# Column sums for the norms by VectorE adds and one full product, and chunks of 512 tokens in panels that feed no norm

## The chip, the cores and the metric

One core of one Trainium2 chip runs the whole program in one launch. The metric is the time on the device in microseconds, as the median of several runs.

## What is computed

Two blocks of a model with 1024 channels over 1024 tokens, all in float32. The first block (with 16 meta tokens in front) mixes by a state space layer and a gated recurrence, and ends in a gated feed-forward net. The second half is two residual layers, "ab" (multiscale pooling and a chunked gating unit) and "cd" (Fourier mixing and attention over the tokens and 256 context tokens). Around the change stand the norms, which need sums over the 1024 channels of each token:

```python
def _layer_norm(x, g, b):
    xf = x.astype(jnp.float32)
    mu = jnp.mean(xf, axis=-1, keepdims=True)
    var = jnp.mean(jnp.square(xf - mu), axis=-1, keepdims=True)
    return ((xf - mu) * lax.rsqrt(var + EPS) * g + b).astype(x.dtype)
...
def _post_norm(x, y, gate, g, b):
    return _layer_norm(ALPHA * x + gate * y, g, b)
...
def rmsnorm(x, g):
    xf = x.astype(jnp.float32)
    y = xf * lax.rsqrt(jnp.mean(xf * xf, axis=-1, keepdims=True) + EPS)
    return (y * g.astype(jnp.float32)).astype(x.dtype)
...
        h = h + merged @ w_out[l]
        z = rmsnorm(h, ffn_norm_g[l])
        u = causal_dwconv(z @ w_up[l], conv_w[l], conv_b[l])
        h = h + (jax.nn.silu(u[..., :D_FF]) * u[..., D_FF:]) @ w_down[l]
    return rmsnorm(h[:, N_META:], final_norm_g)
```

## The kernel before, in words

Activations lie with 128 channels on the partitions and the tokens along the free dimension, so 1024 channels are eight tiles. A product of matrices is made of panels (`panel`): a panel is one output tile of 128 channels, whose columns are cut in chunks of tokens. `CHX` is three chunks of 384, 256 and 384; `CHJ` the same for the 1026 tokens of the first block. For each chunk a PSUM bank is taken from a pool of four (`ps_mm`), 8 (or 4) tiles of the contraction are multiplied into it and an eviction takes the result away. Each factor is kept as a sum of two reduced-precision parts, and each contraction tile costs three matmul instructions (`mm3`, recorded at L83), so a panel of eight tiles is 24 instructions in each chunk, 72 in all. Weights come by DMA and are split in their two parts by ACT (L75) and DVE (L76). Activations are split in the same way by `split_act` (L741, L742).

A sum over channels runs across partitions, so it is a product with ones on PE. `col_sum` gathers the eight source tiles of a chunk in groups of four: each is multiplied with a 32-column matrix of ones (L813), four tiles side by side into one PSUM bank; then ACT copies the bank (L817) and a product with `sel` (L818) adds the four parts and spreads the sum over all partitions. With `tail` set, the last source goes straight into that last bank by a full 128-column product of ones (L808). These products take plain float32 sources, and one of them is recorded as two matmul instructions. Some sums are formed otherwise: `closing` adds the first tiles on DVE into an accumulator (`aacc`, `cacc`, `sqacc`), and with `sq` set (the merge) it uses full products of ones for the accumulator (L779) and for each of the last tiles (L792).

Where the sums are taken:

- **The merge** (`closing` with `sq`, three last panels): the norm in front of the feed-forward net.
- **`ffn.down`, last call**: for each chunk the eight output tiles (L949, evicted with the residual at L951), squared by ACT (L963), a column sum, the reciprocal root (L106 on ACT, L108 to L111 on DVE), and `x1_chunk`, which scales the chunk (L986), modulates it and splits it into `hx`, the input of ab_x. The other nine calls of `down` feed no norm.
- **The context path** (`ctx_path`, 256 tokens): sums of `x` and, in `ln_chunk`, of its squares.
- **ab_x** (`half_out(1)` through `closing`, six last panels, eviction L1309) and **cd_close** (`closing`, seven last panels, eviction L1684): for each chunk the sum of the values, and then `ln_chunk`: mean (L1042), subtraction (L1045), squares (L1047), their column sum, root, and `emit`. The last chunk (`c == 2`) has `tail` set.

What sets the order: the program is written straight on, and a scheduler gives each engine a fixed order of its instructions. Each engine works through its own list, so an instruction that waits holds up all behind it. Products of the next stage or panel are placed between the parts of a sum.

Of the kernel before, what the change touches and what calls it, by code (L numbers as in the profile page):

```python
# [21 lines left out]
CHX = [(0, 384), (384, 640), (640, 1024)]  # L22
NC5 = 130
# [14 lines left out]
class Build:  # L38
# [715 lines left out]
    def closing(self, wsrc, X, nk, chunks, evac, r, sq, acc, tp, done, nres=3, xpool=None, npan=8):  # L754
        nc = self.nc
        n0 = npan - nres
        for i in range(n0):
# [11 lines left out]
            self.panel(w, X, nk, chunks, ev)  # L769
# [5 lines left out]
        for c, (lo, hi) in enumerate(chunks):  # L775
            n = hi - lo
            if sq:
                pc = self.ps_sm()[:, 0:n]
                nc.tensor.matmul(pc, self.ones, acc[:, lo:hi], start=True, stop=False)  # L779
            else:  # L780
                add = self.col_sum(nres + 1, n, lambda: tp.tile([128, 384], F32, tag="mu", name=self.nm("cse"), bufs=1), int(hi == chunks[-1][1]))
                add(0, acc[:, lo:hi])
            for j, (w, o) in enumerate(ws):
# [119 lines left out]
    def ffn(self):  # L903
# [5 lines left out]
        with ExitStack() as es:  # L909
# [32 lines left out]
            def down(js, last):  # L942
# [9 lines left out]
                if not last:  # L952
                    for o in range(8):
                        for lo, hi in CHX:
                            one(o, lo, hi)
                    return
                for c, (lo, hi) in enumerate(CHX):
                    n = hi - lo
                    add = self.col_sum(8, n, lambda: tp.tile([128, 384], F32, tag="cse", name=self.nm("cse"), bufs=1), int(c == 2))
                    for o in range(8):  # L960
                        one(o, lo, hi)
                        t = tp.tile([128, 384], F32, tag="tmp", name=self.nm("sqt"), bufs=6)[:, 0:n]
                        nc.scalar.activation(t, h1[o][:, 2 + lo:2 + hi], AF.Square)  # L963
                        pc = add(o, t)
# [73 lines left out]
    def ln_chunk(self, tp, r, ps, n, emit, sqt, tail):  # L1038
# [4 lines left out]
        add = self.col_sum(8, n, lambda: tp.tile([128, 384], F32, tag="mu", name=self.nm("cse"), bufs=1), tail)  # L1043
        for k in range(8):
# [3 lines left out]
            ps = add(k, t)  # L1048
# [21 lines left out]
    def ab_mixer(self, tp, yp, X, T, chunks, half_out, fill):  # L1070
# [6 lines left out]
        for g, w_ in enumerate((2, 4, 8, 16)):  # L1077
            ap = tile_("ap", T + 16, 2)
# [33 lines left out]
        ys = []  # L1112
# [45 lines left out]
    def ctx_path(self):  # L1158
# [8 lines left out]
        with ExitStack() as es:  # L1167
# [45 lines left out]
            self.ab_mixer(tp, yp, X, T, CH, half_out, fill)  # L1213
# [612 lines left out]
```

## Time and profile before

| what | value |
|---|---|
| median of three runs | 3195.61 us (3192.84 to 3197.05) |
| the profiled execution's own time | 3194.65 us |
| its span | 3192.9 us |
| mean granted TensorE clock | 0.994 |
| PE busy | 3109.1 us (97%) |
| DVE busy | 1830.5 us (57%) |
| ACT busy | 1121.4 us (35%) |

The engines are PE (matmuls), PEld (weight loads, which run beside PE), DVE (VectorE), ACT (ScalarE), POOL (GpSimd) and SP (queues of DMAs). Busy time counts the instructions on an engine; the chain is the work that ended last, followed back from the end step by step to what released it. The granted clock is a share of full speed: 1.00 is 2.4 GHz and 0.50 is 1.2 GHz. A window's row gives each engine's busy time with the number of its instructions. Matmuls overlap in their records, so the price of one is read from the distance between starts, or from a long stretch divided by its count.

### The profile page before, as it was taken

How to read it: one execution, taken by the hardware profiler on the slowest of the kernel's cores; microseconds unless marked ns; L12 is line 12 of the kernel's file. 1: busy time of each engine (PE TensorE's matmuls, PEld its weight loads, DVE VectorE, ACT ScalarE, POOL GpSimd, SP SyncE). 2: the span in 40 equal slices, each digit the busy share in tenths (PEclk: the TensorE clock that was granted, in tenths of full speed). 3: DMA queues.
4: the chain of work that ended last, by engine and by line, in shares of the span. 5: the costliest groups of instructions: out<-in, count | busy, mean ns of one | idle time of the engine just before them, and what ended most of it. 6: DMA issues, size and time to landing. Idle time of an engine off the chain costs nothing.

```text
span 3192.9 us, 47786 instructions
## 1 busy us (share of the span) xinstructions
PE 3109.1 (97%) x19986; PEld 2838.8 (89%) x19986; DVE 1830.5 (57%) x3508; ACT 1121.4 (35%) x1846; POOL 93.1 (3%) x99
## 2 busy tenths in 40 slices
PE   8999899999999999999999999999999999999998
PEld 6999887878999999999999999979999798856576
DVE  7549477776455435365555555555444646688844
ACT  5342642333345312142222122243121535445542
POOL 0000000000210000000000000000000000022100
PEclk9999999999999999999999999999999999999999
DMA  5352445343452234211111111101111314200111
GB/s 158 89 163 94 141 170 168 113 139 108 142 170 93 63 129 132 67 40 48 48 50 41 47 53 47 47 24 59 47 50 37 104 61 136 90 4 11 67 63 53
DMA packets 106384, 269.01 MB, mean 84 GB/s; under 512 B 14798, under 2 KB 43694, under 8 KB 105974
## 3 DMA queue, kind: packets, MB, share of 16 engines
q1 hardware_dynamic: 99656, 245.35, 23.6%
q10 hardware_dynamic: 4464, 16.34, 1.3%
q0 software_dynamic: 2048, 4.26, 0.6%
q8 instruction: 157, 2.57, 0.3%
q14 instruction: 59, 0.48, 0.0%
HBM read 219.12 MB, written 46.11 MB: 83 GB/s over the span
## 4 chain that ended last, share of the span: by engine, by line
PE 87%; DVE 6%; ACT 3%; DMA 3%; issue 1%; SPq 0%; DVEq 0%; ACTq 0%
PE mm L83 63%; PE mm L949 7%; PE mm L1567 3%; PE sm L813 2%; PE sm L1555 2%; PE mm L1124 2%; DMA YBd<-o 1%; PE sm L1531 1%; ACT Tt L502 1%; DVE R L604 1%; PE sm L465 1%; DMA wm<-ab_w_mod 0%; PE sm L708 0%; PE sm L1017 0%; PE sm L687 0%
## 5 line engine op out<-in xcount | busy, mean ns | idle before, releaser
L83 PE MATMUL mm<-z,whl 128*128 128x256 f32 (+3 forms) x4032 | 684.5, 325 | 1.9 <-ACT z L231 1.0
L83 PE MATMUL mm<-a,whl 128*128 128x384 f32 (+1 forms) x4320 | 682.6, 319 | 1.6 <-ACT u L917 1.6
L83 PEld LDWEIGHTS mm<-a,whl 128*128 128x128 f32 x4320 | 678.5, 188 | 3.7 <-ACT u L917 1.9
L83 PEld LDWEIGHTS mm<-z,whl 128*128 128x128 f32 x4032 | 639.1, 190 | 36.0 <-issue 29.2
L76 DVE TENSOR_TENSOR whl<-wraw,whl 128x1024 fp32r<-128x1024 f32 (+2 forms) x258 | 302.8, 1179 | 224.5 <-ACT whl L75 223.7
L75 ACT CAST whl<-wraw 128x1024 fp32r<-128x1024 f32 (+2 forms) x258 | 260.6, 1015 | 342.1 <-PE mm L949 136.9
L83 PE MATMUL mm<-hx,whl 128*128 128x384 f32 (+1 forms) x2232 | 365.4, 322 | 7.7 <-ACT fx L1378 7.1
L83 PEld LDWEIGHTS mm<-hx,whl 128*128 128x128 f32 x2232 | 351.2, 189 | 16.8 <-ACT fx L1378 7.3
L949 PEld LDWEIGHTS mm<-g,whl 128*128 128x128 f32 x1584 | 248.0, 188 | 13.9 <-issue 8.1
L949 PE MATMUL mm<-g,whl 128*128 128x384 f32 (+1 forms) x1584 | 257.9, 322 | 2.3 <-DVE f L951 1.2
L83 PE MATMUL mm<-b,whl 128*128 128x384 f32 (+1 forms) x1152 | 180.9, 319 | 0.0
L83 PEld LDWEIGHTS mm<-b,whl 128*128 128x128 f32 x1152 | 180.8, 189 | 0.0
L917 ACT COPY u<-mm 128x384 f32<-128x384 f32 x132 | 58.4, 445 | 317.9 <-PE mm L83 317.9
L951 DVE TENSOR_TENSOR f<-f,mm 128x384 f32<-128x384 f32 (+1 forms) x240 | 118.4, 509 | 71.3 <-PE mm L949 70.4
L83 PEld LDWEIGHTS mm<-y,whl 128*128 128x128 f32 x816 | 119.9, 188 | 13.0 <-issue 9.8
L83 PE MATMUL mm<-y,whl 128*128 128x256 f32 (+1 forms) x816 | 127.8, 312 | 1.3 <-ACT y L741 1.0
L1567 PE MATMUL mm<-m,KB 97*128 97x512 f32 x420 | 118.2, 401 | 1.3 <-ACT P L1568 1.3
L1568 ACT ACTIVATE P<-mm 128x512 f32<-128x512 f32 x160 | 91.5, 596 | 68.6 <-PE mm L1567 50.9
L1532 DVE TENSOR_REDUCE mx<-sm 128x1 f32<-128x512 f32 (+1 forms) x192 | 103.8, 596 | 15.6 <-PE sm L1531 14.6
L1567 PEld LDWEIGHTS mm<-m,KB 97*128 97x128 f32 x420 | 76.9, 191 | 24.9 <-issue 7.3
L923 DVE TENSOR_SCALAR av<-u,conv_w,conv_b 128x1024 f32<-128x1024 f32 x22 | 17.9, 812 | 138.9 <-ACT u L917 138.9
L923 DVE TENSOR_SCALAR ag<-u,conv_w,conv_b 128x1024 f32<-128x1024 f32 x22 | 17.9, 813 | 119.1 <-ACT u L917 119.1
(519 smaller groups left out, 3729.9 us busy)
## 6 DMA issues: line engine op xcount, KB each, us to landing
wraw<-w_up SPq DMA_DIRECT2D x44, 512.0 KB, 3.2
wraw<-w_h SPq DMA_DIRECT2D x32, 512.0 KB, 3.4
wraw<-ab_w SPq DMA_DIRECT2D x32, 512.0 KB, 3.3
wm<-ab_w_mod SPq DMA_DIRECT2D x24, 512.0 KB
wm<-cd_w_mod SPq DMA_DIRECT2D x24, 512.0 KB, 4.8
wraw<-w_down SPq DMA_DIRECT2D x22, 512.0 KB, 3.2
ut<-Ud SPq DMA_DIRECT2D x16, 520.0 KB, 4.0
gt<-Gd SPq DMA_DIRECT2D x16, 513.0 KB, 3.2
```

Of the source, the lines that this page charges most:

```text
L75: self.nc.scalar.copy(t[:, 0], raw)
L76: self.nc.vector.tensor_tensor(out=t[:, 1], in0=raw, in1=t[:, 0].bitcast(F32), op=ALU.subtract)
L83: nc.tensor.matmul(ps, W[:, wp, wofs + 128 * k:wofs + 128 * k + 128], X(xp, kofs + k, lo, hi), start=first and k == 0 and i == 0, stop=las ...
L813: nc.tensor.matmul(p4[32 * j:32 * j + 32], self.ones[:, 0:32], x, start=i < 4, stop=i - len(pend) + j + 5 >= m)
L917: return u, (self.split_w(A["w_up"][p], [1024]), lambda c, lo, hi, ps: nc.scalar.copy(u[:, lo:hi], ps))
L949: nc.tensor.matmul(ps, ws[j][:, wp, 128 * o:128 * o + 128], G[j][:, xp, lo:hi], start=n_ == 0 and i == 0, stop=n_ == len(js) - 1 and i == 2)
L951: v.tensor_tensor(out=h1[o][:, 2 + lo:2 + hi], in0=h1[o][:, 2 + lo:2 + hi], in1=ps, op=ALU.add)
L1124: nc.tensor.matmul(ps, X(xp, k, 128 * t, 128 * t + 128), wv[k // 4][:, wp, 256 * (k % 4):256 * (k % 4) + 256], start=k == 0 and i == 0, st ...
L1532: v.tensor_reduce(out=mx[:, qt, j:j + 1], in_=ps, axis=mybir.AxisListType.X, op=ALU.max)
L1555: mm = nc.tensor.matmul(po[64 * c:64 * c + 64, :], vv(t)[:, 64 * h:64 * h + 64], P[t][:, c], start=t == 0, stop=t == KT - 1)
L1567: nc.tensor.matmul(ps, K[0:97, kp, 128 * t:128 * t + 128], Q[0:97, qp, 512 * c:512 * c + 512], start=i == 0, stop=i == 2)
L1568: E[t] = nc.scalar.activation(Pt[:, c], ps, AF.Exp, scale=scale)
```

## The change

Two edits. First, sums over the channels are added up on DVE and go through one full product of ones for each chunk: in `closing` (all last tiles are added to the accumulator; in the last chunk the last tile goes straight into the product's bank), in the last `ffn.down` (the squares are added into `cse`), in `ln_chunk` except for the last chunk and the first block, and in the context path's sum of values. Second, panels that feed no norm are cut in two chunks of 512 (`CH5`): in ab_x the pooling panels 1 to 3, the second half's eight and the first output half; the panels of `closing` ahead of its last ones; the nine inner calls of `down`; gates 1 to 7; three Fourier panels; two query panels; and the four of the Fourier output.

```diff
@@ closing
-    def closing(self, wsrc, X, nk, chunks, evac, r, sq, acc, tp, done, nres=3, xpool=None, npan=8):
+    def closing(self, wsrc, X, nk, chunks, evac, r, sq, acc, tp, done, nres=3, xpool=None, npan=8, wide=None):
...
-            self.panel(w, X, nk, chunks, ev)
+            self.panel(w, X, nk, wide or chunks, ev)
...
-            if sq:
-                pc = self.ps_sm()[:, 0:n]
-                nc.tensor.matmul(pc, self.ones, acc[:, lo:hi], start=True, stop=False)
-            else:
-                add = self.col_sum(nres + 1, n, lambda: tp.tile([128, 384], F32, tag="mu", name=self.nm("cse"), bufs=1), int(hi == chunks[-1][1]))
-                add(0, acc[:, lo:hi])
...
-                    nc.tensor.matmul(pc, self.ones, t, start=False, stop=i == npan - 1)
-                else:
-                    pc = add(j + 1, src)
+                    src = t
+                if i == npan - 1 and hi == chunks[-1][1]:
+                    nc.tensor.matmul(pc, self.ones, src, start=False, stop=True)
+                    continue
+                nc.vector.tensor_tensor(out=acc[:, lo:hi], in0=acc[:, lo:hi], in1=src, op=ALU.add)
+                if i == npan - (2 if hi == chunks[-1][1] else 1):
+                    pc = self.ps_sm()[:, 0:n]
+                    nc.tensor.matmul(pc, self.ones, acc[:, lo:hi], start=True, stop=i == npan - 1)
@@ ffn.down
-                        for lo, hi in CHX:
+                        for lo, hi in CH5:
                             one(o, lo, hi)
...
-                    add = self.col_sum(8, n, lambda: tp.tile([128, 384], F32, tag="cse", name=self.nm("cse"), bufs=1), int(c == 2))
+                    tot = tp.tile([128, 384], F32, tag="cse", name=self.nm("cse"), bufs=1)[:, 0:n]
...
-                        t = tp.tile([128, 384], F32, tag="tmp", name=self.nm("sqt"), bufs=6)[:, 0:n]
+                        t = tp.tile([128, 384], F32, tag="tmp", name=self.nm("sqt"), bufs=6)[:, 0:n] if o else tot
                         nc.scalar.activation(t, h1[o][:, 2 + lo:2 + hi], AF.Square)
-                        pc = add(o, t)
+                        if o == 7 and c == 2:
+                            nc.tensor.matmul(pc, self.ones, t, start=False, stop=True)
+                            continue
+                        if o:
+                            v.tensor_tensor(out=tot, in0=tot, in1=t, op=ALU.add)
+                        if o == (6 if c == 2 else 7):
+                            pc = self.ps_sm()[:, 0:n]
+                            nc.tensor.matmul(pc, self.ones, tot, start=True, stop=o == 7)
@@ ln_chunk
-            ps = add(k, t)
+            if tail:
+                ps = add(k, t)
+            elif k == 0:
+                t0 = t
+            else:
+                v.tensor_tensor(out=t0, in0=t0, in1=t, op=ALU.add)
+        if not tail:
+            ps = self.ps_sm()[:, 0:n]
+            nc.tensor.matmul(ps, self.ones, t0, start=True, stop=True)
@@ ctx_path
-            add = self.col_sum(8, T, lambda: tp.tile([128, 384], F32, tag="mu", name=self.nm("cse"), bufs=1))
-            for k in range(8):
-                ps = add(k, x[:, k])
...
+            tot = sqs[:, 0]
+            v.tensor_tensor(out=tot, in0=x[:, 0], in1=x[:, 1], op=ALU.add)
+            for k in range(2, 8):
+                v.tensor_tensor(out=tot, in0=tot, in1=x[:, k], op=ALU.add)
+            ps = self.ps_sm()[:, 0:T]
+            nc.tensor.matmul(ps, self.ones, tot, start=True, stop=True)
@@ gate, and alike in fourier, latents' input, the Fourier output, ab_mixer and half_out(0)
-        self.panel(w, X, 8, CHX, ev)
+        self.panel(w, X, 8, CH5, ev)
```

How the order moves is shown at three places. A row is an instruction in an engine's order, with its number there, the line, output and inputs, the shape and how many alike follow in a row (`f`: the residual; `hx`: ab_x's input; `mm`, `sm`: PSUM banks). The line numbers of the changed kernel run 1 to 22 ahead of those of before.

First, PE at the end of the FFN's last `down`, before:

```order
4575 L813 MATMUL sm_19587<-sqt_19671,ones 32x384
4576 L813 MATMUL sm_19587<-sqt_19687,ones 32x384
4577 L949 MATMUL mm_19711<-g_18997,whl_19191 128x384
4578 L813 MATMUL sm_19587<-sqt_19703,ones 32x384
4579 L949 MATMUL mm_19711<-g_18997,whl_19191 128x384
4580 L949 MATMUL mm_19711<-g_19178,whl_19196 128x384 x3
4581 L83 MATMUL mm_19808<-hx_19351,whl_19803 128x384 x2
4582 L83 MATMUL mm_19834<-hx_19351,whl_19803 128x256
4583 L818 MATMUL sm_19588<-cse_19708,sel 128x384
4584 L83 MATMUL mm_19834<-hx_19351,whl_19803 128x256
4585 L83 MATMUL mm_19808<-hx_19351,whl_19803 128x384
4586 L808 MATMUL sm_19588<-sqt_19725,ones 128x384
```

and in the changed kernel:

```order
4384 L951 MATMUL mm_19115<-g_18094,whl_18602 128x384 x3
4385 L951 MATMUL mm_19115<-g_18413,whl_18607 128x384 x3
4386 L951 MATMUL mm_19115<-g_18594,whl_18612 128x384 x3
4387 L84 MATMUL mm_19212<-hx_18763,whl_19207 128x384
4388 L973 MATMUL sm_19113<-cse_18995,ones 128x384
4389 L967 MATMUL sm_19113<-sqt_19129,ones 128x384
4390 L84 MATMUL mm_19212<-hx_18763,whl_19207 128x384 x2
```

The 32-column products among L949 (now L951) are gone. The full products of the sum (L973 for `cse`, L967 for the last square) now stand behind one product of the next stage.

Second, DVE at the same place, before:

```order
2402 L742 TENSOR_TENSOR hx_19355<-hx_19568,hx_19355 128x256
2403 L742 TENSOR_TENSOR hx_19356<-hx_19573,hx_19356 128x256
2404 L951 TENSOR_TENSOR f_13003<-f_13003,mm_19673 128x384
2405 L742 TENSOR_TENSOR hx_19357<-hx_19578,hx_19357 128x256
2406 L742 TENSOR_TENSOR hx_19358<-hx_19583,hx_19358 128x256
2407 L951 TENSOR_TENSOR f_13034<-f_13034,mm_19689 128x384
2408 L951 TENSOR_TENSOR f_13065<-f_13065,mm_19711 128x384
2409 L76 TENSOR_TENSOR whl_19803<-wraw_19804,whl_19803 128x1024
2410 L76 TENSOR_TENSOR whl_19887<-wraw_19888,whl_19887 128x1024
2411 L108 TENSOR_SCALAR rsm_19730<-sm_19588 128x384
2412 L109 TENSOR_TENSOR rsm_19730<-rsm_19730,rsy_19728 128x384
2413 L110 TENSOR_TENSOR rsm_19730<-rsm_19730,rsy_19728 128x384
```

and in the changed kernel:

```order
2367 L953 TENSOR_TENSOR f_13024<-f_13024,mm_19096 128x384
2368 L953 TENSOR_TENSOR f_13055<-f_13055,mm_19115 128x384
2369 L743 TENSOR_TENSOR hx_18769<-hx_18986,hx_18769 128x256
2370 L743 TENSOR_TENSOR hx_18770<-hx_18991,hx_18770 128x256
2371 L970 TENSOR_TENSOR cse_18995<-cse_18995,sqt_19025 128x384
2372 L970 TENSOR_TENSOR cse_18995<-cse_18995,sqt_19042 128x384
2373 L970 TENSOR_TENSOR cse_18995<-cse_18995,sqt_19059 128x384
2374 L970 TENSOR_TENSOR cse_18995<-cse_18995,sqt_19076 128x384
2375 L970 TENSOR_TENSOR cse_18995<-cse_18995,sqt_19093 128x384
2376 L970 TENSOR_TENSOR cse_18995<-cse_18995,sqt_19110 128x384
2377 L77 TENSOR_TENSOR whl_19207<-wraw_19208,whl_19207 128x1024
2378 L77 TENSOR_TENSOR whl_19291<-wraw_19292,whl_19291 128x1024
```

Six adds (L970) now stand between the last evictions (L953) or splits (L743) and the weight splits (L77) and root (L109).

Third, DVE in ab_x's closing, in the last chunk, before:

```order
2696 L1045 TENSOR_TENSOR f_13065<-f_13065,mu_22719 128x256
2697 L1309 SCALAR_TENSOR_TENSOR f_12803<-mm_22821,mod_ab,f_12803 128x384
2698 L1309 SCALAR_TENSOR_TENSOR f_12897<-mm_22835,mod_ab,f_12897 128x384
2699 L1309 SCALAR_TENSOR_TENSOR f_13003<-mm_22853,mod_ab,f_13003 128x384
2700 L1309 SCALAR_TENSOR_TENSOR f_13034<-mm_22867,mod_ab,f_13034 128x384
2701 L76 TENSOR_TENSOR whl_23020<-wraw_23021,whl_23020 128x1024
2702 L76 TENSOR_TENSOR whl_23026<-wraw_23027,whl_23026 128x1024
2703 L108 TENSOR_SCALAR rsm_22756<-sm_22722 128x256
2704 L1309 SCALAR_TENSOR_TENSOR f_13065<-mm_22886,mod_ab,f_13065 128x384
```

and in the changed kernel, the same evictions (now L1331):

```order
2660 L1063 TENSOR_TENSOR sqt_21587<-sqt_21587 128x256
2661 L793 TENSOR_TENSOR aacc<-aacc,f_12701 128x384
2662 L1063 TENSOR_TENSOR sqt_21587<-sqt_21587,sqt_21593 128x256
2663 L1331 SCALAR_TENSOR_TENSOR f_12795<-mm_21681,mod_ab,f_12795 128x384
2664 L1063 TENSOR_TENSOR sqt_21587<-sqt_21587,sqt_21593 128x256
2665 L793 TENSOR_TENSOR aacc<-aacc,f_12795 128x384
2666 L1063 TENSOR_TENSOR sqt_21587<-sqt_21587,sqt_21600 128x256
2667 L1331 SCALAR_TENSOR_TENSOR f_12889<-mm_21696,mod_ab,f_12889 128x384
2668 L1063 TENSOR_TENSOR sqt_21587<-sqt_21587,sqt_21600 128x256
2669 L793 TENSOR_TENSOR aacc<-aacc,f_12889 128x384
2670 L1063 TENSOR_TENSOR sqt_21587<-sqt_21587,sqt_21607 128x256
2671 L1331 SCALAR_TENSOR_TENSOR f_12993<-mm_21711,mod_ab,f_12993 128x384
```

The evictions stood together, and now adds for this chunk's values (L793) and for the squares of the second chunk (L1063) stand between them. Ahead of them, between the eviction of `f_12701` and that of `f_12795`, stand 30 rows of the first two chunks' norms.

## Rows read from the trace of the kernel before

**Rows 1.** The page, parts 1 and 4: busy time by engine; the chain by engine.
```profile
PE 3109.1 (97%) x19986; PEld 2838.8 (89%) x19986; DVE 1830.5 (57%) x3508; ACT 1121.4 (35%) x1846; POOL 93.1 (3%) x99
...
PE 87%; DVE 6%; ACT 3%; DMA 3%; issue 1%; SPq 0%; DVEq 0%; ACTq 0%
```

**Rows 2.** Chain in order of time, stretches of products alone: start us, us, what.
```profile
1350.81 4.21 PE mm L83 x24
...
1477.52 22.78 PE mm L949 x144
...
2295.54 22.41 PE mm L1124 x192
...
2648.75 11.16 PE mm L1419 x48
...
2724.06 11.24 PE mm L83 x72
```

**Rows 3.** PE's timeline in the FFN's last down: start us, us, instructions.
```profile
2112.09 0.83 PE L813 MATMUL sm<-sqt,ones 128*32 128x384 f32 x2
2112.86 0.86 PE L949 MATMUL mm<-g,whl 128*128 128x256 f32 x5
2113.55 0.86 PE L818 MATMUL sm<-cse,sel 128*128 128x384 f32 x2
2113.95 2.25 PE L949 MATMUL mm<-g,whl 128*128 128x256 f32 x15
```

**Rows 4.** Windows, stages E, A, B, C, D: us, PE, PEld, DVE, ACT, POOL busy (x), PEclk.
```profile
970.40:981.50 11.10, 11.10 (x67) 6.57 (x68) 4.39 (x12) 5.46 (x13) 0.00 (x0) 1.00 0.00 0
1343.80:1403.90 60.10, 58.49 (x337) 54.47 (x336) 38.58 (x75) 23.72 (x44) 0.00 (x0) 1.00 0.10 35
2097.30:2155.40 58.10, 56.36 (x308) 42.52 (x308) 30.71 (x66) 30.17 (x64) 0.00 (x0) 1.00 0.03 7
2455.10:2520.30 65.20, 65.20 (x350) 45.25 (x349) 39.92 (x86) 32.10 (x68) 0.00 (x0) 1.00 0.19 65
...
3081.00:3171.90 90.90, 90.85 (x521) 71.87 (x520) 28.87 (x61) 18.72 (x40) 0.00 (x0) 1.00 0.08 30
```

**Rows 5.** PE's groups by line and shape, 2097.2 to 2155.4: busy us, mean ns | idle before.
```profile
L949 PE MATMUL mm<-g,whl 128*128 128x384 f32 x152 | 31.3, 350 | 1.5 <-DVE f L951 1.2 <-DVE g L742 0.3
L949 PE MATMUL mm<-g,whl 128*128 128x256 f32 x96 | 12.5, 287 | 0.0
```

**Rows 6.** DVE's timeline: two dependent operations, then eight independent ones.
```profile
2116.45 0.55 DVE L108 TENSOR_SCALAR rsm<-sm 128x384 f32<-128x384 f32 x1
2117.04 0.56 DVE L109 TENSOR_TENSOR rsm<-rsm,rsy 128x384 f32<-128x384 f32 x1
...
2467.35 3.84 DVE L1045 TENSOR_TENSOR f<-f,mu 128x384 f32<-128x384 f32 x8
```

**Rows 7.** Windows, inside and behind PE's longest idle stretch, same columns.
```profile
2529.00:2532.00 3.00, 0.00 (x0) 0.00 (x0) 3.00 (x8) 2.97 (x7) 0.00 (x0) 0.50 0.70 256
2532.00:2536.00 4.00, 3.52 (x18) 3.52 (x19) 1.14 (x5) 2.94 (x6) 0.00 (x0) 0.56 0.93 272
```

**Rows 8.** PE's groups of products, 2455.0 to 2520.4, same columns.
```profile
L83 PE MATMUL mm<-y,whl 128*128 128x384 f32 x110 | 22.3, 348 | 0.0
L83 PE MATMUL mm<-y,whl 128*128 128x256 f32 x72 | 11.3, 297 | 0.0
L83 PE MATMUL mm<-hx,whl 128*128 128x384 f32 x54 | 10.7, 348 | 0.0
...
L83 PE MATMUL mm<-hx,whl 128*128 128x256 f32 x13 | 3.0, 320 | 0.0
```

**Rows 9.** PE's timeline at that idle stretch; in brackets idle us and its releaser.
```profile
2532.48 0.80 PE L83 MATMUL mm<-hx,whl 128*128 128x256 f32 x2 [7.11 <-ACT fx L1378]
```

**Rows 10.** PE's timeline at the start of the last chunk of the last down.
```profile
2125.91 3.07 PE L949 MATMUL mm<-g,whl 128*128 128x384 f32 x16 [1.20 <-DVE f L951]
```

More of the change, by code (lines that the diff above doesn't have):

```diff
@@ L22 @@
 CHX = [(0, 384), (384, 640), (640, 1024)]
+CH5 = [(0, 512), (512, 1024)]
 NC5 = 130
@@ L1042, in ln_chunk @@
         v.tensor_scalar(out=mu, in0=ps, scalar1=1.0 / 1024, scalar2=None, op0=ALU.mult)
-        add = self.col_sum(8, n, lambda: tp.tile([128, 384], F32, tag="mu", name=self.nm("cse"), bufs=1), tail)
+        if tail:
+            add = self.col_sum(8, n, lambda: tp.tile([128, 384], F32, tag="mu", name=self.nm("cse"), bufs=1), tail)
         for k in range(8):
@@ L1047, in ln_chunk @@
             nc.scalar.activation(t, r(k), AF.Square)
-            ps = add(k, t)
+            if tail:
+                ps = add(k, t)
[6 more added lines that the diff above has]
+            nc.tensor.matmul(ps, self.ones, t0, start=True, stop=True)
         rs = self.rsqrt(tp, ps, n, 1.0 / 1024, EPS / ALPHA ** 2)
@@ L1068, in ab_consts, with ab_mixer @@
         nc.sync.dma_start(self.sgb, A["sgu_b"].partition_broadcast(128))
-    def ab_mixer(self, tp, yp, X, T, chunks, half_out, fill):
+    def ab_mixer(self, tp, yp, X, T, first, wide, half_out, fill):
         nc, A = self.nc, self.A
@@ L1077, in ab_mixer @@
         for g, w_ in enumerate((2, 4, 8, 16)):
+            chunks = wide if g else first
             ap = tile_("ap", T + 16, 2)
@@ L1111, in ab_mixer @@
         half_out(0, ys)
-        ys = []
+        ys, chunks = [], wide
         nt = T // 128
@@ L1212, in half_out @@
                     self.panel(w, Y, 4, CH, ev)
-            self.ab_mixer(tp, yp, X, T, CH, half_out, fill)
+            self.ab_mixer(tp, yp, X, T, CH, CH, half_out, fill)
             self.abg, self.abb = self.load(self.const, "ab_ln_g"), self.load(self.const, "ab_ln_b")
@@ L1220, in emit @@
                 self.split_act(H[:, :, k], 0, T, d)
-            add = self.col_sum(8, T, lambda: tp.tile([128, 384], F32, tag="mu", name=self.nm("cse"), bufs=1))
-            for k in range(8):
-                ps = add(k, x[:, k])
             sqs = cp.tile([128, 4, T], F32, name="csq")
-            self.ln_chunk(tp, lambda k: x[:, k], ps, T, emit, lambda k: sqs[:, k % 4], 0)
+            tot = sqs[:, 0]
[4 more added lines that the diff above has]
+            nc.tensor.matmul(ps, self.ones, tot, start=True, stop=True)
+            self.ln_chunk(tp, lambda k: x[:, k], ps, T, emit, lambda k: sqs[:, 1 + (k - 1) % 3 if k else 0], 0)
             for _ in range(16):
@@ L1314, in half_out @@
                 if which:
-                    self.closing(ws, Y, 4, CHX, ev, self.rx, False, acc, tp, done, nres=6)
+                    self.closing(ws, Y, 4, CHX, ev, self.rx, False, acc, tp, done, nres=6, wide=CH5)
                 else:
@@ L1320, in half_out @@
                         w = w2[:, :, 512 * (i % 2):512 * (i % 2) + 512]
-                        self.panel(w, Y, 4, CHX, lambda c, lo, hi, ps: ev(i, c, lo, hi, ps))
-            self.ab_mixer(tp, yp, X, 1024, CHX, half_out, lambda: None)
+                        self.panel(w, Y, 4, CH5, lambda c, lo, hi, ps: ev(i, c, lo, hi, ps))
+            self.ab_mixer(tp, yp, X, 1024, CHX, CH5, half_out, lambda: None)
     def cd_x(self):
@@ L1379, in fourier @@
             if h:
-                self.panel(w, X, 8, CHX, ev)
+                self.panel(w, X, 8, CH5, ev)
             else:
@@ L1404, in fourier @@
             x = tp.tile([128, 1024], F32, tag="x", name=self.nm("cq"))
-            self.panel(w, X, 8, CHX, lambda c, lo, hi, ps: nc.scalar.copy(x[:, lo:hi], ps))
+            self.panel(w, X, 8, CH5, lambda c, lo, hi, ps: nc.scalar.copy(x[:, lo:hi], ps))
             cq.append(x)
@@ L1613, in mla @@
                     w = self.split_w(A["fnet_w"][i], [512])
-                    self.panel(w, Y, 4, CHX, lambda c, lo, hi, ps: tt(out=gt[:, lo:hi], in0=ps, in1=gt[:, lo:hi], op=ALU.mult))
+                    self.panel(w, Y, 4, CH5, lambda c, lo, hi, ps: tt(out=gt[:, lo:hi], in0=ps, in1=gt[:, lo:hi], op=ALU.mult))
                     nc.sync.dma_start(self.ycd[i], gt)
@@ L1697, in done @@
                 self.ln_chunk(tp, lambda k: rr[k][:, lo:hi], ps, hi - lo, emit, sqt, int(c == 2))
-            self.closing(A["cd_wo"], self.acc_fn(ys), 8, CHX, ev, lambda i, lo, hi: rr[i][:, lo:hi], False, acc, tp, done, nres=7, xpool=wx)
+            self.closing(A["cd_wo"], self.acc_fn(ys), 8, CHX, ev, lambda i, lo, hi: rr[i][:, lo:hi], False, acc, tp, done, nres=7, xpool=wx, wide=CH5)
 def pk(a):
```

## The prediction

> **What bounds the kernel now.** I read the page's busy shares and its chain first. TensorE (PE) is busy 97% of the span and holds 87% of the chain that ended last; VectorE (DVE) holds 6% [rows 1]. So a change pays by what it takes off PE, as long as PE is not made to wait instead. The second view is the chain in order of time, at stretches of nothing but products [rows 2]. They show the price of a product by its width: 24 of 384 columns in 4.21 us are 0.1753 us each, 192 of 256 in 22.41 are 0.1167, 48 of 512 in 11.16 are 0.2325. Per column these agree to half a per cent, so a wide chunk saves no column time; what it can save is the changes of chunk. The third view is PE's timeline inside a sum [rows 3]. Between the start of the 32-column products at 2112.09 and the next L949 at 2112.86 lie 0.77 us for two instructions that stream 384 columns. The full-width product L818 at 2113.55 holds PE 0.40 us until 2113.95 (two instructions too), although it streams as much.
>
> I then measured five stages around the sums by windows [rows 4]: A, the merge's closing (1343.8 to 1403.9); B, the FFN's last down with its norm (2097.3 to 2155.4); C, ab_x's closing with its norm (2455.1 to 2520.3); D, cd_close (3081.0 to 3171.9); E, the context norm (970.4 to 981.5). In all of them PE is nearly full at a granted clock of 1.00, while DVE is busy 38.58 of 60.10, 30.71 of 58.10, 39.92 of 65.20, 28.87 of 90.90 and 4.39 of 11.10 us. That is the room for the adds: ample in D, thin in B and C once PE's part shrinks.
>
> **The prices of the new work.** A DVE add of 384 columns is taken from two rows: eight independent ones in 3.84 us, 0.48 each, and dependent ones that start 0.59 apart (2116.45 and 2117.04) [rows 6]. The adds into one accumulator depend on each other, so 0.59 holds where they stand in a row and 0.48 where other work lies between. For 256 columns I estimate two thirds of these and a little more, 0.34 to 0.44. A full product costs PE 0.40 at 384 columns [rows 3] and by the same proportion some 0.3 at 256.
>
> **Stage D, −9.2 us.** Seven panels run in the last pass, each 24 products in each of three chunks: 7 × 24 × (2 × 0.1753 + 0.1167) = 78.5 us by rows 2, of 90.9 [rows 4]. So 12.4 us are the sums' visits and copies. Left are six full products, 2.2 us, and I add 1.0 us for the last chunk, where eviction and one add now stand in front of the product. DVE gets 34 adds here, some 17 us on its 28.9 in a stage of over 80: covered by PE's products. If that cover were gone they would show as waits of PE on L1684's evictions, at most those 17 us. Bounds −7 to −10.2. The tail behind 3171.9 keeps its column sums and is unchanged.
>
> **Stage B, −8.7 us.** The window holds 152 products of 384 and 96 of 256 columns of L949 [rows 5] and six of the next stage: 26.6 + 11.2 + 0.9 = 38.8 us of 58.1; 19.3 are lost, of them 1.2 to a wait on DVE [rows 10] and 0.5 to one on a weight split. After, four full products take 1.5. DVE gets 20 adds, and where they stand decides. In the first two listings of the order PE meets the last sum's product behind a single product of the next stage, and on DVE the six adds that it waits for stand in a row behind the whole of the second chunk's emission and the last evictions; the root's steps and the next stage's weight splits come behind them. So PE stands while DVE works off 6 × 0.59 = 3.5 us of adds and some 2 us of emission ahead of them: 5.5 us. I add 2 us at the start of the third chunk, where the evictions wait behind the first chunk's emission as they do now (1.2). That makes 38.8 + 1.5 + 5.5 + 2 = 47.8, a gain of 10.3. The idle stretch has a price: in the one long idle stretch of this kernel [rows 9] the granted clock falls to 0.50, and the four microseconds behind it run at 0.56 with PE busy 3.52 [rows 7], so 3.52 × 0.44 = 1.55 us are lost. I charge that: −8.7. Bounds −4 (all of the adds in a row on the path) to −11.
>
> **Stage C, −8.0 us.** Here the products are 164 × 0.1753 + 85 × 0.1167 = 38.7 us of 65.2 [rows 8]. The last chunk keeps its column sum (some 5.9 us with its copies, by the 0.77 of rows 3 and the final two products), six full products come in (2.2), so PE alone could be done in 46.8. But DVE had 39.9 us and gets 31 adds, 13 × 0.55 + 13 × 0.42 + 5 × 0.55 = 15.4, together 55.3. DVE becomes the pace. The third listing shows it: between the first and the second eviction of the last chunk DVE now has 30 rows of the first two chunks' norms, and adds between the other evictions, and PE, which has four banks for products, must stop until they are emptied. 65.2 − 55.3 is 9.9; less one fall of the clock, 1.55, it is −8.3, and I take −8.0 because the longer wait on fx, 7.11 now [rows 9], falls with a stretch of the same DVE queue. Bounds −3 (DVE's adds all at 0.59, with gaps) to −18.
>
> **Stage E, −2.3 us.** In the window PE ran 67 instructions, 36 of them in the two sums; the other 31 of 256 columns are 3.6 us, so 7.5 are lost. In their place stand two chains of seven adds at 0.34 to 0.44, of which the first delays the mean. Most of the gain goes there; I keep a third. Bounds 0 and −6.
>
> **Stage A, −1.5 us.** Twelve full products become four: eight times 0.40 or 0.3, 3.0 us on PE. The path behind the sum (root, DVE, ACT) is unchanged, and PE's idle time of 1.6 in front of its next products (60.10 less 58.49) [rows 4] grows, so up to half goes back. Bounds 0 and −3.
>
> **Wide chunks, −4.8 us.** Counted in the order of both kernels, 1650 products of 512 columns take the place of 1650 of 384 and 825 of 256 at L83: 34.4 panels of 48. Such a panel of 72 takes 11.24 us now [rows 2]; 48 of 512 take 11.16. That is 34.4 × 0.08 = 2.8 us. A down of the FFN takes 22.78; its columns alone are 96 × 0.1753 + 48 × 0.1167 = 22.43, so the 24 changes of group cost 0.015 each. With 16 groups and 96 × 0.2325 it is 22.56: 0.22 less, nine times 2.0. Longer evictions are off the path, since one bank in four is emptied while 5 us of products run. Bounds −2 to −6.5. A rule gives another number: the Trainium skill (TensorE: Matmul & The Clock Gate, Back-to-back issue gap) has a lone product take its columns at 2.4 GHz and 2.5 ns more; the 1257 products that fall away would then give 3.1 us, an estimate by that page. Its 216 ns for 512 columns differs from the 232.5 of rows 2, so the rows decide.
>
> **The sum.** −9.2 − 8.7 − 8.0 − 2.3 − 1.5 − 4.8 = −34.5. The profiled execution took 3194.65 us, 0.96 below the median of the three runs, so 3160.1 by the profile and **3161 us** on the median. A measurement of this kernel can tell about 0.2% from no change, 6.4 us.
>
> **The rivals.** (1) *DVE takes more of it*: B and C are already paced by DVE, B gives 4 and C nothing. For it speaks that DVE's total would fill 40.8 of 47.8 us in B; against, that its idle time now is spread over the evictions, where adds can slip in. −9.2 − 4 − 2.3 − 1.5 − 4.8 = −21.8: 3174. With the wide chunks and E at their low ends, 3178. (2) *The visits come off whole*: the adds hide and no new wait shows. A 3, B 17, C 18, D 10, E 6 and wide 6.5 make −60: 3135; the two orders speak against it. (3) *Slower, by DVE's queue in B and C*: each add ends up in the chain, B's 20 for 7 × 0.59 + 7 × 0.44 + 6 × 0.59 = 10.8 and C's 31 for 16.4, nothing of PE's saving there is kept, and three falls of the clock cost 4.7: +31.9 against −17.8 from D, E, A and the wide chunks, 3210. It decides from the point where every eviction of B and C waits on the queue; now DVE holds 6% of the chain and PE waits 1.2 us on an eviction in B [rows 1, 10], which speaks against it. (4) *The clock*: each new idle stretch brings a fall. A rule that speaks against this change stands in the Trainium skill (TensorE: Matmul & The Clock Gate, HAM oscillation): waits between bursts of products let each burst start at 1.2 GHz. The trace agrees, 0.50 in its one long wait [rows 7]. I have charged two; with falls also in A, E and twice more in C, 4 × 1.55 = 6.2 us, it would be 3167, inside the forecast's own bounds. That the change does not do what it says can be left out: the order shows PE with 6231 rows in place of 6802.
>
> **The chances.** The forecast 0.58, rival 4 0.10, rival 1 0.18, rival 2 0.10, rival 3 0.04. The range takes in the bounds of the stages and rival 1, and leaves out the far part of rival 2 and all of rival 3: 3145 to 3180. Faster 0.93; the same 0.04, from rival 1 with a weak D, and slower 0.03.
>
> **What would show it.** In the trace after: D's stage some 9 us shorter with no L1684 wait; in B, a PE wait of 4 to 7 us in front of the last sum's product, released by a DVE add; in C, DVE busy near 90% and PE waiting on its evictions; 144 products of a down gone to 96 in 22.5 us. If DVE stays under 75% in B and C and PE does not wait, rival 2 is right; if C's stage is as long as before, rival 1. A down that takes over 22.8 us, or any stage that is longer, would prove the forecast wrong.

## The result, and the profile after

The changed kernel takes 3151.72 us (median of four runs, 3150.20 to 3154.40), the kernel before beside it 3194.23 us. The ratio is 0.9865 with a 95% interval of 0.9849 to 0.9881: 1.35% faster, 42.5 us. Forecast were 3161 us in a range of 3145 to 3180. The profiled execution has a span of 3149.7 us in place of 3192.9 and a mean granted clock of 0.989 in place of 0.994.

The page after, parts 1 and 4, against [rows 1]:

```profile
PE 3045.6 (97%) x18485; PEld 2714.6 (86%) x18485; DVE 1864.8 (59%) x3517; ACT 1110.4 (35%) x1802; POOL 93.2 (3%) x99
...
PE 85%; DVE 8%; ACT 4%; DMA 3%; issue 1%; SPq 0%; DVEq 0%; ACTq 0%
```

PE lost 63.5 us of busy time and the span only 43.2: PE now waits more, and DVE's share of the chain rose from 6% to 8%.

Stages are compared here (`ups` are the FFN's products with `w_up`, `downs` the calls of `ffn.down`) between points that both traces have (the start of a certain run of products), since the first 930 us, which the change does not touch, differ by some us from one execution to the next: the same L1143 run starts at 930.52 us in this profile and at 924.99 in another of the same program. The stretches are: the FFN's end (from the last 288 up products to ab_x's first run of 192 in its second half; it holds B), ab_x's end (from the second such run to the first later panel pair of one width; it holds C), cd_close (from the last sum of the attention to the last panel's eviction; it holds D). The stretches of B and C hold some wide panels too.

| stretch, us | before | after | gain | forecast |
|---|---|---|---|---|
| context norm and merge (E, A), from the context path's run of 48 products to the first up products | 475.13 | 473.28 | 1.9 | 3.8 |
| the first ups behind the merge | 73.65 | 75.04 | -1.4 | (in A) |
| nine downs | 9 x 22.78 | 9 x 22.41 | 3.3 | 2.0 |
| FFN's end (B) | 251.93 | 243.80 | 8.1 | 8.7 |
| ab_x's end (C) | 231.16 | 220.96 | 10.2 | 8.0 |
| cd_close (D) | 116.39 | 95.38 | 21.0 | 9.2 |

The downs and a pair of plain panels, in the chain in order of time, against [rows 2]:

```profile
1403.80 75.04 PE mm L84 x480
1478.84 22.41 PE mm L951 x96
...
2307.72 22.18 PE mm L84 x96
```

and a pair of panels in three chunks, in the kernel before:

```profile
2317.95 22.48 PE mm L83 x144
```

A down takes 22.41 in place of 22.78. Two panels of eight tiles take 22.18 (a pair in three chunks took 22.48), 0.15 us less for each where the forecast had 0.08.

cd_close, in the chain from its first sum to its last panel:

```profile
3035.16 41.92 PE mm L84 x227
3077.08 0.86 PE sm L796 x2
3077.94 8.56 PE mm L84 x72
...
3086.56 0.88 PE sm L1066 x2
3087.45 11.38 PE mm L84 x92
3098.83 0.52 PE sm L796 x2
...
3125.16 0.82 PE sm L796 x2
3125.98 2.82 PE mm L84 x16
...
3128.82 0.63 DVE m L1706
```

Between the sums stand unbroken runs of products; PE waits for nothing until the last eviction. Of the 93.6 us from 3035.16 to the last product, 78.5 are the last pass and 11.1 the first panel; some 4 are left for the sums, five full products in the chain. The chain of the kernel before, at the same place:

```profile
3057.21 23.86 PE mm L83 x143
3081.08 0.78 PE sm L813 x6
```

There 143 products are recorded ahead of the first sum: the 72 of the first panel, and the first chunk of three panels of the last pass, which is 72 more.

The FFN's end on PE and DVE (timelines; in brackets the idle time ahead):

```profile
2142.96 0.69 PE L84 MATMUL mm<-hx,whl 128*128 128x384 f32 x1 [4.43 <-ACT whl L76]
2143.65 1.65 PE L973 MATMUL sm<-cse,ones 128*128 128x384 f32 x2
...
2145.80 4.45 PE L84 MATMUL mm<-hx,whl 128*128 128x384 f32 x18
```

```profile
2139.06 0.76 DVE L743 TENSOR_TENSOR hx<-hx,hx 128x256 fp32r<-128x256 f32 x2
2139.73 3.87 DVE L970 TENSOR_TENSOR cse<-cse,sqt 128x384 f32<-128x384 f32 x6
2143.51 2.35 DVE L77 TENSOR_TENSOR whl<-wraw,whl 128x1024 fp32r<-128x1024 f32 x2
```

PE stands for 4.43 us in front of the first product of ab_x, which the profile puts down to the cast of its weights on ACT. DVE's six adds run from 2139.73 to 2143.60, and the full product of the sum follows at 2143.65, so both chains end within 0.7 us of each other. The idle stretch at the merge, ahead of the first ups, was 1.6 us before (60.10 less 58.49 [rows 4]) and is now 5.05:

```profile
1403.80 6.41 PE L84 MATMUL mm<-a,whl 128*128 128x258 f32 x40 [5.05 <-ACT u L919]
```

Windows behind the idle stretches of the merge and of the FFN (us, busy of PE, PEld, DVE, ACT, POOL, granted clock):

```profile
1403.80:1407.00 3.20, 3.20 (x15) 3.20 (x16) 0.03 (x1) 1.08 (x3) 0.00 (x0) 0.51 0.00 0
2143.00:2147.00 4.00, 4.00 (x7) 2.39 (x8) 2.83 (x3) 1.24 (x2) 0.00 (x0) 0.50 0.07 17
2443.00:2501.50 58.50, 45.42 (x247) 39.50 (x246) 51.63 (x115) 30.14 (x64) 0.00 (x0) 0.88 0.20 66
```

Behind both, PE runs at half clock (0.51 and 0.50) for 3 to 4 us. The third row is ab_x's closing and norm: DVE is busy 51.63 of 58.50 us, 88%. PE's waits there:

```profile
2478.25 4.11 PE L84 MATMUL mm<-y,whl 128*128 128x384 f32 x12 [5.85 <-DVE f L1331]
...
2494.69 3.97 PE L815 MATMUL sm<-sqt,ones 128*32 128x384 f32 x14 [4.82 <-ACT sqt L1057]
...
2513.20 7.01 PE L84 MATMUL mm<-hx,whl 128*128 128x256 f32 x54 [1.90 <-ACT fx L1400]
```

It waits 5.85 us for an eviction that stands behind the first chunk's norm on DVE and 4.82 for the last chunk's squares. Behind each the granted clock falls, to 0.50 (2478.25 to 2482.00) and 0.58 (2495 to 2500). The wait on fx fell from 7.11 to 1.90 [rows 9].

### The profile page after: what moved, and what is told of

Its sections match the earlier page's. It is cut to its first block, busy times and chain, and to the rows that moved or that the text cites. A ratio compares the mean times of both kernels' runs of the same rounds, so it can differ in the third digit from the quotient of the medians.

```text
span 3149.7 us, 44789 instructions
## 1 busy us (share of the span) xinstructions
PE 3045.6 (97%) x18485; PEld 2714.6 (86%) x18485; DVE 1864.8 (59%) x3517; ACT 1110.4 (35%) x1802; POOL 93.2 (3%) x99
## 4 chain that ended last, share of the span: by engine, by line
PE 85%; DVE 8%; ACT 4%; DMA 3%; issue 1%; SPq 0%; DVEq 0%; ACTq 0%
PE mm L84 62%; PE mm L951 7%; PE mm L1589 3%; PE sm L1577 2%; PE mm L1143 2%; DMA YBd<-o 2%; PE sm L1553 1%; DVE R L605 1%; ACT Tt L503 1%; PE sm L466 1%; DVE B L600 1%; PE sm L709 0%; PE sm L815 0%; PE sm L688 0%; DVE F L599 0%
## 5 line engine op out<-in xcount | busy, mean ns | idle before, releaser
L77 DVE TENSOR_TENSOR whl<-wraw,whl 128x1024 fp32r<-128x1024 f32 (+2 forms) x258 | 302.7, 1177 | 214.4 <-ACT whl L76 214.0
L84 PE MATMUL mm<-hx,whl 128*128 128x512 f32 (+2 forms) x1608 | 358.3, 380 | 6.3 <-ACT whl L76 4.4
L84 PEld LDWEIGHTS mm<-hx,whl 128*128 128x128 f32 x1608 | 290.9, 189 | 63.9 <-ACT whl L76 4.7
L951 PE MATMUL mm<-g,whl 128*128 128x512 f32 (+2 forms) x1152 | 251.8, 379 | 2.9 <-DVE f L953 1.8
L951 PEld LDWEIGHTS mm<-g,whl 128*128 128x128 f32 x1152 | 208.3, 189 | 43.0 <-DVE f L953 2.0
L953 DVE TENSOR_TENSOR f<-f,mm 128x512 f32<-128x512 f32 (+2 forms) x168 | 108.8, 660 | 55.7 <-PE mm L951 55.6
L84 PE MATMUL mm<-y,whl 128*128 128x256 f32 (+2 forms) x687 | 124.8, 340 | 8.3 <-DVE f L1331 7.5
L84 PEld LDWEIGHTS mm<-y,whl 128*128 128x128 f32 x687 | 109.9, 190 | 21.5 <-DVE f L1331 8.0
```

What stands on the lines that cost most here:

```text
L77: self.nc.vector.tensor_tensor(out=t[:, 1], in0=raw, in1=t[:, 0].bitcast(F32), op=ALU.subtract)
L84: nc.tensor.matmul(ps, W[:, wp, wofs + 128 * k:wofs + 128 * k + 128], X(xp, kofs + k, lo, hi), start=first and k == 0 and i == 0, stop=las ...
L951: nc.tensor.matmul(ps, ws[j][:, wp, 128 * o:128 * o + 128], G[j][:, xp, lo:hi], start=n_ == 0 and i == 0, stop=n_ == len(js) - 1 and i == 2)
L953: v.tensor_tensor(out=h1[o][:, 2 + lo:2 + hi], in0=h1[o][:, 2 + lo:2 + hi], in1=ps, op=ALU.add)
```

## The experiments

The theory behind the first four: PE's time goes to the lone 32-column products, and most of the gain is that they are gone. The rivals: it is the change between forms of the array that costs, or the wide chunks carry the gain.

**e1: the sums alone.** `CH5 = CHX` in the changed kernel.

> The changed kernel with its new sums, and all panels in the old three chunks. Theory: read at the same points of the two traces, the stages give E 1.2, B 6.6, C 9.1 and D 20.9 us, and the merge loses 0.7, so the sums alone are worth 37 us and the time is about 3157. Rival: the wide chunks carry a third of the gain or more; then about 3166 or above.

Measured: 3157.31 us, ratio 0.9893 (0.9878 to 0.9908), 35.4 us less than before. **e2: the wide chunks alone**, in the kernel before.

> The kernel before with the wide chunks alone, sums as they were. Theory: the remaining 7.7 us of the gain are theirs, 3.4 in the nine downs (22.78 to 22.41 each) and the rest in the panels (22.48 to 22.18 for two), so about 3186.5. The forecast's term said 4.8 (3189.5). Rival: they are worth something only beside the new sums, then under 3 us (3191.5 or above).

Measured: 3183.91 us, ratio 0.9976 (0.9967 to 0.9986), 8.8 us. The parts add up to the whole (44.2 us against 42.5) as far as the medians can tell, and the sums carry four fifths. In e1's stretches, FFN's end is 243.74, ab_x's end 222.07 and cd_close 95.54; in e2's 250.23, 230.36 and 116.20.

**e3: every source by a full product**, in the kernel before, behind the first block:

```diff
+        if self.full:
+            pf = self.ps_sm()[:, 0:n]
+            def one(i, src):
+                nc.tensor.matmul(pf, self.ones, src, start=i == 0, stop=i == ns - 1)
+                return pf
+            return one
```

> The kernel before, in which every source of a column sum behind the first block goes through its own full 128-column product of ones: no 32-column products, no copy, no sel, and no adds. Theory: a lone 32-column product costs what it streams, about 0.70 us at 384 columns, and only some 0.2 to 0.3 for the change of form; then the full ones save 0.2 to 0.3 for each of some 110 sources and the copies, D gains about 6 us, all stages about 16, time about 3178. Rival, the price of the forecast: a full product costs 0.40, so D gains 12, all stages about 30, time about 3164.

Measured: 3179.09 us, ratio 0.9957 (0.9942 to 0.9972), 13.6 us. The time is the theory's, but it did not come as the theory had it: cd_close gained 0.4 us only (115.99), so neither number was right there, and ab_x's end gained 8.2 (222.92). The chain of e3, in cd_close:

```profile
3069.87 0.75 PE sm L809 x2
3070.62 4.19 PE mm L84 x24
3074.81 0.76 PE sm L809 x2
...
3092.30 5.76 PE sm L809 x18
...
3109.42 2.85 PE mm L84 x24
...
3121.24 4.24 PE sm L809 x18
```

A full product costs the chain 0.76 us at 384 columns and 0.57 at 256, no less than a lone 32-column product (0.76 and 0.55, shown below). So the price comes neither from the change of form nor from the number of output columns: it is one more stream of float32 columns, 0.76 us or more than four of the products at 0.1753. That it stands alone is a small part: the two runs of nine (eight of 384 columns and one of 256, then eight of 256 and one of 384) give 0.66 and 0.45 for each. The forecast's 0.40 [rows 3] was too low. The chain of the kernel before gives the same L818 0.70 us:

```profile
2113.71 0.70 PE sm L818 x2
```

so in the timeline of rows 3 the next start is recorded before the product is paid for.

**e7: the four 32-column products of a group in one run**, in the kernel before; the last source's product goes first and the others are ordered behind it:

```diff
-                for j, x in enumerate(pend):
-                    nc.tensor.matmul(p4[32 * j:32 * j + 32], self.ones[:, 0:32], x, ...)
+                first = None
+                for j in [len(pend) - 1] + list(range(len(pend) - 1)):
+                    mm = nc.tensor.matmul(p4[32 * j:32 * j + 32], self.ones[:, 0:32], pend[j], ...)
+                    if first is not None:
+                        self.tc.add_manual_dep(mm.ins, first.ins.name, ...)
+                    first = first or mm
```

> The kernel before, its 32-column products kept, but the four of a group put one behind the other in PE's order, behind the last of the four sources. Theory: the four sit in different columns of the array and stream side by side, so four cost about what a lone one does, 1.0 us at 384 columns; D then gains about 15 us, B 10, C 9, all together 34 to 38, time about 3158, close to the sums by adds. Rival: each 32-column product is paid for itself wherever it stands; then under 6 us from the changes of form alone, 3189 or above.

Measured: 3158.44 us, ratio 0.9893 (0.9876 to 0.9909), 34.3 us. The chain of e7 in cd_close, and of the kernel before:

```profile
3083.69 0.78 PE sm L814 x8
...
3107.01 0.57 PE sm L814 x8
```

```profile
3106.68 0.76 PE sm L813 x2
...
3131.88 0.55 PE sm L813 x2
```

Four sources (eight instructions) cost 0.78 us at 384 columns where one source alone (two instructions) cost 0.76. Side by side they are nearly free; the kernel before lost that because the order put products between them. Without a single new add on DVE the median is almost that of e1. In cd_close it gains 12.4 us (104.02) against 20.9, since it still pays two runs and a `sel` product for each sum; in the FFN's end (244.34) and ab_x's end (222.13) it stands level with the adds. These three stretches give 29.0 us, where e1 has 38.2. Another 6.8 us of the trace's gain lie ahead of the context path's 48 products (921.97 in place of 928.73). This edit reaches the first block's sums too, but kernels that leave that block as it was differ there by as much (923.65 to 930.52), so that part is not shown to be the edit's. In ab_x's end e3 and e7 gain alike, but PE's wait on fx, 7.11 us before [rows 9], is nearly gone in e3 and stands in e7 (first e3, then e7):

```profile
2519.75 18.60 PE L84 MATMUL mm<-hx,whl 128*128 128x256 f32 x120 [0.33 <-ACT fx L1387]
```

```profile
2506.47 20.93 PE L83 MATMUL mm<-hx,whl 128*128 128x256 f32 x120 [7.68 <-ACT fx L1383]
```

**a0: the changed kernel again**, on the chip of the next three.

> The changed kernel once more, beside the three kernels that are made from it. Expected as before: 3152, within 0.1%.

Measured: 3148.77 us, ratio 0.9858 (0.9844 to 0.9873). **e4: the changed kernel with cd_close's sums as before.**

> The changed kernel with the sums of cd_close (values and squares) as they were before, all else changed. Theory: D alone carries 20.9 us, since the old stage lost 24.8 us to its sums; time about 3172.5. Rival, the forecast's step for D: 9.2 us, time about 3161, and the other 12 us came from somewhere else.

Measured: 3167.98 us, ratio 0.9919 (0.9902 to 0.9936), 19.2 us above a0; cd_close takes 116.22 us in place of 95.38, 20.8 us. That stage alone carries half of the gain. **e5: the changed kernel with the merge's sums as before.**

> The changed kernel with the merge's sums (twelve full products) as they were. Theory: the chain of DVE and ACT behind the last sum sets the merge's end, PE's 3 us only lengthen its idle time (5.1 in place of 1.6), and the fall of the clock behind it goes away: 0.7 us faster than the changed kernel, 3151. Rival, the forecast's step: 1.5 us slower, 3153.2.

Measured: 3150.78 us, ratio 0.9862 (0.9847 to 0.9877), no difference that the medians can show from a0. In the trace PE's wait at the merge's end is 1.6 us again, and the ups behind it take 73.66 in place of 75.04 to 75.51: the fall of the clock is gone, as the theory had it. But the stretch ahead of the ups takes 475.23 in place of 473.28 to 473.61. The merge's part of the change is worth nothing that shows.

**e6: evictions first.** As e5, with the evictions of `closing`'s last pass at high priority.

> As the kernel with the merge's old sums, and the evictions of the last pass of closing at high priority in DVE's order, so that none waits behind the norm of an earlier chunk. Theory: PE's wait of 5.9 us for an L1331 eviction in C goes, and C ends 3 to 6 us earlier: about 3147. Rival: DVE is full from the first chunk to the last, so its work is only put in another order and the root of the last chunk comes when it did: 0 to 1 us, about 3151.

Measured: 3157.88 us, ratio 0.9885 (0.9870 to 0.9900): slower than either theory expected. The wait for the eviction is gone, and a longer one stands elsewhere (PE's waits; us in total, times, longest):

```profile
PE sm L1090 <- DVE sqt L1087: 11.0, 1, 11.0
PE mm L84 <- ACT fx L1424: 7.6, 1, 7.6
```

PE waits 11.0 us at one product for the second chunk's squares, whose adds were pushed back, and 7.6 at fx; ab_x's end takes 227.72, against 220.80 in e5. Here, with DVE 88% busy, another order moved the wait and made it longer.

**e8 and e9: what paces the ends of B and C.** e8 leaves out the modulation on ACT, e9 the adds on DVE, in the FFN's last norm and in ab_x's.

> The changed kernel without the modulation (scale and shift) between the norm and the split, in the FFN's last norm and in ab_x's: the split is taken from the normed value itself, which leaves out 8 ACT operations for each of six chunks (four of the last eight on DVE). All sums and adds stay. Theory: what ends B and C now is the emission of the norms on ACT, which stands in the chain in front of the last chunk's squares; B's hx restart comes some 4 us earlier and C some 6 to 8 us, about 3138 to 3141. Rival: DVE's queue with the adds ends them; ACT's work is beside it, and the time stays within 2 us of the changed kernel's.

> The changed kernel without the new adds of the FFN's last norm and of ab_x's closing and norm (51 adds): the product of each sum is taken of its last source alone, so these means and roots are of one tile. Theory: the adds lie beside ACT's emission for the most part; B gains under 1 us and C some 2 to 4, about 3146 to 3149. Rival, the forecast's step for C: DVE is the pace, and without 25 us of adds B and C end 10 us or more earlier, 3139 or below.

Measured: 3144.31 us, ratio 0.9854 (0.9837 to 0.9870), and 3139.72, ratio 0.9841 (0.9825 to 0.9858). By stretches: without modulation the FFN's end is 241.54 (2.3 us less) and ab_x's end 220.96 (the same). In e8's FFN's end the wait in front of the last sum is gone, but the eviction at the start of the third chunk is waited for 4.4 us, 1.79 in the changed kernel:

```profile
PE mm L951 <- DVE f L953: 4.4, 1, 4.4
```

Without the adds the FFN's end is 235.36, 8.4 us less, so the theory fell there: the adds on DVE hold up B, and far more than ACT's modulation does. In ab_x's end PE restarts at fx 4.5 us earlier against the same point (153.03 in place of 157.53), but the stretch is only 1.7 us shorter (219.24). The trace of e9 shows the rest:

```profile
2485.46 6.63 PE L85 MATMUL mm<-hx,whl 128*128 128x384 f32 x42
2497.66 21.34 PE L85 MATMUL mm<-hx,whl 128*128 128x256 f32 x120 [5.57 <-ACT fx L1404]
```

PE is through with its products earlier and stands 5.57 us at fx, as it did before the change.

**e10: 28 of the adds on GpSimd**, with the merge's sums as before.

> The changed kernel with the merge's old sums, and with GpSimd in place of DVE for 28 of the new adds: the FFN norm's of the first two chunks (14) and those of the squares in ab_x's norm (14). GpSimd is idle there; its adds of 1024 columns take 2.48 us in the attention, so some 0.95 at 384 and 0.63 at 256. Theory, from the run without these adds (B 8.5 us shorter, ab_x's closing 4.5): they stand in DVE's queue in front of evictions and splits, so with GpSimd B gets 3 to 6 us shorter and the closing 1 to 3, some of it given back by the clock; about 3145. Rival: a chain of GpSimd adds ends later than DVE's did, and roots and all behind them come later: 3152 or above.

Measured: 3163.50 us, ratio 0.9910 (0.9893 to 0.9926): the rival's side. The FFN's end was 244.25, as with DVE, and ab_x's end 233.04, 12 us more. GpSimd's groups by line and shape (busy us, mean ns):

```profile
L994 POOL TENSOR_TENSOR cse<-cse,sqt 128x384 f32<-128x384 f32 x7 | 7.1, 1012 | 1170.8 <-ACT sqt L989 1170.6
...
L1087 POOL TENSOR_TENSOR sqt<-sqt,sqt 128x256 f32<-128x256 f32 x6 | 5.8, 970 | 0.5
```

An add of 384 columns takes 1.01 us and one of 256 in ab_x 0.97, where DVE's mean in the changed kernel is 0.56 and 0.41, and PE waited 5.3 us for such a chain.

**e11: full products where PE stands idle.** As e5, with the squares of the FFN's last chunk each through a full product:

```diff
-                        if o == 7 and c == 2:
-                            nc.tensor.matmul(pc, self.ones, t, start=False, stop=True)
+                        if c == 2:
+                            if o == 0:
+                                pc = self.ps_sm()[:, 0:n]
+                            nc.tensor.matmul(pc, self.ones, t, start=o == 0, stop=o == 7)
                             continue
...
```

> The changed kernel with the merge's old sums, and with the squares of the last chunk of the FFN's last down each through its own full product (eight), in place of six adds in a row on DVE and two products. Theory: PE stands idle for 4.4 us in front of this sum, so the products take time that is there, DVE has 3.9 us less in front of the weight splits, and the clock does not fall: from the first product of the last FFN group's ups to ab_x's first L1143 stretch it takes some 3 us less than in the changed kernel (243.8), so about 3148 in all. Rival: ACT's squares and weight split end the stage anyway, and the eight products, 0.7 us each, come on top: 0 to 3 us longer, 3151 to 3154.

Measured: 3146.87 us, ratio 0.9863 (0.9846 to 0.9880). The stretch takes 241.34 in place of 243.80 (a0: 244.05; e5, which has the same squares as the changed kernel: 242.28), so 1 to 3 us less:

```profile
2132.33 4.78 PE L992 MATMUL sm<-sqt,ones 128*128 128x384 f32 x14 [0.18 <-ACT sqt L988]
2136.65 13.57 PE L84 MATMUL mm<-hx,whl 128*128 128x384 f32 x82
```

Seven products (14 instructions) run while ACT squares, and PE goes on at 2136.65 without a break; the windows behind show a granted clock of 1.00. It has the lowest span of the versions that leave nothing out, 3140.9 us, but of its 8.8 us below the changed kernel's only the 1 to 3 us in the stretch are the edit's: 6.9 lie ahead of the context path's 48 products (923.65 in place of 930.52). The medians can't tell it from the changed kernel.

## Why the prediction was right, and where it was not

- **The whole** was right: faster, by the removal of lone column sums from PE (e1, e4), and the time in the range. It came out 9 us below the forecast. One stage, D, gave 11.8 us more than its term, and more than its own bounds of −7 to −10.2 allowed; the wide chunks gave some 4 more, A and E together 3.3 less. That the range held all the same is luck as far as D goes: the bounds of the other terms left the room.
- **Stage D was mis-sized: 21.0 us where −9.2 stood.** The step that failed is the count: "Seven panels run in the last pass, each 24 products in each of three chunks" = 78.5 us, taken from a window of 90.9. The window began at the first sum, and the first chunk of three of those panels, 72 products or some 12.6 us, had run ahead of it (the run of 143 from 3057.21 to 3081.08). So the sums lost 25 us, not 12.4. The count in the window's own row would have shown it: 504 products and the 88 instructions of the sums' 39 sources and five `sel` products make 592, and the row has 521 [rows 4].
- **The full product's 0.40 us was wrong**, 0.57 to 0.76 by e3, and the chain of before had 0.70 for the same instruction. It cost little, since few are left.
- **Stage B was right in size and mostly in mechanism**: 8.1 to 8.2 us (after, e1) for −8.7, although the stretch also holds wide panels, which gave 1.7 us there in e2, and kernels with the same sums run from 242.28 to 244.05. The wait in front of the last sum was forecast at 5.5 us and is 4.43, with the fall of the clock behind it; the one at the third chunk was forecast at 2 and is 1.79. The releaser of the 4.43 us is ACT's weight cast in the trace and not a DVE add, as the forecast's sign wanted it; the last add ends only 0.6 us later. That the adds are on the path is shown by e9.
- **Stage C was right in size, and only in part in mechanism.** It gained 10.2 us with 0.8 of the wide chunks (e2), 9.1 in e1, for −8.0. DVE at 88% and the wait on the eviction were as forecast, but the clock fell twice where one fall was charged, and its fall at fx [rows 7], not reckoned with, went. And three different ways of forming the sums (e1, e3, e7) shorten it by 9.1, 8.2 and 9.0, two of them without a new add. They do so in different ways: in e3 the wait on fx is nearly gone, and in e7 it stands, 10 us earlier. So "DVE becomes the pace" is not shown for C's end: without DVE's adds (e9) it gives 4.5 us up to fx and 1.7 in all, without ACT's modulation (e8) nothing. What ends C stays open.
- **Stages A and E**: −1.5 and −2.3 were forecast. E gave 1.2 us (65.50 to 64.34 from the 48 products to the next long run), A 0.7 up to the merge's end, and the ups behind took 1.4 longer. So A came out 0.7 us longer in the trace, which the prediction had named as a sign of being wrong. The step that failed is "up to half goes back": PE's wait grew from 1.6 to 5.05 us, more than the 3 us that were saved, and the fall of the clock came on top. The rival of the clock was right for A: e5 shows the fall gone.
- **Wide chunks**: 4.8 forecast, 8.8 by e2's median. The downs alone gave 3.3 for 2.0: the 16 groups of a down cost 0.09 us beside 96 × 0.2325, not 16 × 0.015. A panel gave 0.15 for 0.08, so 34.4 of them 5.2 us, and the two make 8.5. By rows e2's stretches and downs account for 6.6; another 2.5 lie between ab_x's end and cd_close (455.34 in place of 457.85).
- **The rivals**: DVE's bound (1) holds in B as a limit on what is left, not as a loss; the visits coming off nearly whole (2) is true in D alone; the slower side (3) did not come. The clock (4) came close to what that rival describes: new falls stand in A, in B, twice in C and in E (0.50 from 988 to 990 us), where two were charged, and the old one at fx went. Stage D's surplus more than covered them.

## What to carry to other kernels

Where a sum over partitions is formed by products, count the streams of columns that the source type needs and not the output columns: a lone narrow product costs as much as a full one, and only products that run side by side are cheap. Taking them off the matrix engine paid nearly in full where nothing else is near full (cd_close, 21 of 25 us), and by half or less where the adds land in a queue that evictions and splits share (8 of the 19 us that B lost beside its products, 10 of C's 26). There the same sums gathered on the matrix engine did as well (e7), and its idle time can take some of them (e11, 1 to 3 us in the trace). Before a window is used as a stage, count the instructions that should be in it.

## What was not expected of the hardware

- Four 32-column products of different sources, in a row, cost the chain 0.78 us at 384 columns, as one does (0.76); a full 128-column one also costs 0.76 alone and 0.66 in a row of eight (e3, e7).
- A wait of 5 us costs more than itself: behind it PE ran at 0.50 to 0.51 of its clock for 3 to 4 us, and 480 products took 1.4 us longer (after against e5).
- GpSimd's adds of 256 columns took 0.75 us in the FFN, with DVE busy 1.33 of the 5.80 us, and 0.97 in ab_x's norm, with DVE busy 4.88 of 6.30 (e10). That the two disturb each other was not tried.
